# A chunked delta rule on one core: the triangular inverse kept as full 128x128 blocks in place of 64x64 blocks, and a solve as one product in place of three

## The chip, the core and the metric

The kernel runs on one core of one Trainium2 chip. TensorE (PE) multiplies matrices, VectorE (DVE) and ScalarE (ACT) do elementwise work and read its results out of PSUM, GpSimd (POOL) does small elementwise work in SBUF, and SyncE (SP) issues the loads. The metric is the device time of one execution in microseconds; lower is better.

## What is computed

Two layers of a trunk over 256 tokens of width 1024, in float32. Each layer has a SwiGLU block, a mixer and another SwiGLU block, with norms around them. The mixer of layer 0 is a short convolution; that of layer 1 is a gated delta rule with 16 value heads of 128 columns. The part that matters here is the delta rule. The reference works in chunks of 64 tokens:

```
a = where(strict, einsum("bhncd,bhnsd->bhncs", k_beta, k) * decay, 0.0)
t_inv = lax.linalg.triangular_solve(eye + a, broadcast_to(eye, a.shape), left_side=True, lower=True)
u = einsum("bhncs,bhnse->bhnce", t_inv, v_beta)
w = einsum("bhncs,bhnsd->bhncd", t_inv, k_beta * exp(g)[..., None])
...
v_new = u_n - einsum("bhcd,bhde->bhce", w_n, state)
o = einsum("bhcd,bhde->bhce", q_g_n, state) + einsum("bhcs,bhse->bhce", qk_n, v_new)
state = state * exp(gl_n) + einsum("bhcd,bhce->bhde", k_tail_n, v_new)
```

The result doesn't depend on where a chunk ends, so the kernel takes one chunk of 128 tokens: two chunks (t = 0, 1) and 16 heads, in 4 groups (gi) of 4 heads.

## The kernel before

**Products.** The large products are float32, done as two or three products of rounded halves: `unit` loads a 128x1024 piece of a weight (SP), rounds it on ACT (L111, `whi`) and takes the rest on DVE (L113, `wlo`). In the delta mixer `stat_group` (L247 to L249) makes q, k and v, `act_group` (L216, L217, L220) makes the gate z, and `out_proj` (L288 to L290) the last product. The products of the delta rule itself are plain float32 products; in the trace each of them is two passes on PE.

**Order.** Each of these groups calls `tk.tick()` every 6 or 12 matmuls. A ticker then resumes the generators that are due: `kq_chain`, `invert`, `v_pair`, one `scan` for each group gi, and `z_chain`. A generator that yields n is resumed n ticks later, so that its instructions stand between those of the weight products. A scheduler in the compiler then moves a few rows past one that it thinks would wait. An engine runs its list in order.

**The matrix.** `kq_chain` leaves for each gi and t a tile `KQ[gi][t]` of 128x4x2x128 elements: for each of 4 heads the decayed key-key matrix (index 0 of the third axis, upper triangular as stored) and the decayed key-query matrix (index 1). The 32x32 blocks on the diagonal are copied to `Ld`.

**The inverse.** `invert` inverts all 32 x 4 diagonal blocks of 32x32 at once by forward substitution on DVE (L635, L637), which gives them as `Xd` and, transposed, `Yd` (L639, L641). After `INV_WAIT` ticks it goes on in two halves of 16 matrices: 32 products of 32x32 with the block beside the diagonal (L652), a copy (L656, into `T1`), a tick, 32 more products (L663), and then the tiles `Y64[gi]`: the inverses of the 64x64 diagonal blocks, put together from copies of `Yd` and zeros on POOL (L669, L671) and from PSUM on ACT (L673).

**The solve.** `scan(gi)` waits for v and for `Y64[gi]`, and solves twice, for t = 0 and 1, with other products between. `solve` does it by 64x64 blocks: both diagonal blocks (L704, 8 products of 64x64 by 64x128, whose results ACT copies, L706); two ticks; the block beside them (L710, 4 products, ACT copy L713); two ticks; the second diagonal block again (L718, 4 products), subtracted by DVE (L719); two ticks. What follows in `scan` and `intra` (L726, L757, L766) is of 128 rows.

## Time and profile before

| what | value |
|---|---|
| median of three runs | 1145.38 us (1145.0 to 1147.21) |
| the profiled execution, its own time | 1144.5 us |
| span of its profile | 1142.8 us |
| PE busy | 1108.3 us (97%) |
| DVE busy | 759.1 us (66%) |
| ACT busy | 652.4 us (57%) |
| POOL busy | 80.3 us (7%) |
| mean granted TensorE clock | 0.994 of 2.4 GHz |
| mean rate of the loads | 174 GB/s |

The profile is of one execution, and 1.7 us of its time lie outside the span. Matmuls are pipelined: one that is listed with 0.28 us starts 0.12 us after the one before it. What an instruction costs PE is therefore read from the start of one row to the start of the next, in the view in order of time, and not from its length. The inversion and the solves lie between about 815 and 930 us.

### The profile page before, as it was taken

To read this page: it belongs to the slowest core of one execution; us is meant where nothing else is said; L and a number is where in the kernel's file an instruction comes from. 1 tells how busy PE (TensorE), PEld (TensorE's weight loads), DVE (VectorE), ACT (ScalarE), POOL (GpSimd) and SP (SyncE) were. 2 spreads that over 40 slices of the span, in tenths; PEclk is the share of its full clock that TensorE was granted. 3 is DMA by queue.
4 is the path that set the end of the run, shared out by engine and by line. 5 is a ranking of instruction groups with operands and counts; after the bars stand their busy time and mean duration, and the time that the engine had idled before them with its cause. 6 is when DMAs were issued, how large, how long until landed. Compare 5 with 4: busy or idle time off the path is not lost.

```text
span 1142.8 us, 16740 instructions
## 1 busy us (share of the span) xinstructions
PE 1108.3 (97%) x6272; PEld 942.5 (82%) x6272; DVE 759.1 (66%) x1145; ACT 652.4 (57%) x1187; POOL 80.3 (7%) x145
## 2 busy tenths in 40 slices
PE   6999999999999999999999999988999999999997
PEld 5888887788788888788888887867998877888886
DVE  5686735687776764667674479778865567767543
ACT  5766635545565653556563468874676545656432
POOL 1000000000200000010000012210210212000000
PEclk9999999999999999999999999999999999999999
DMA  7765555665566555566655543346434145665552
GB/s 259 232 210 193 195 162 165 225 183 195 176 225 204 174 197 167 175 215 202 200 176 171 183 157 111 95 141 189 146 97 160 43 132 169 221 197 180 189 166 74
DMA packets 55953, 198.64 MB, mean 174 GB/s; under 512 B 6720, under 2 KB 7232, under 8 KB 55872
## 3 DMA queue, kind: packets, MB, share of 16 engines
q1 hardware_dynamic: 55872, 197.58, 53.9%
q8 instruction: 49, 0.80, 0.3%
q14 instruction: 32, 0.26, 0.1%
HBM read 196.51 MB, written 1.05 MB: 173 GB/s over the span
## 4 chain that ended last, share of the span: by engine, by line
PE 81%; DVE 6%; ACT 5%; DMA 3%; issue 2%; POOL 2%; SPq 0%; DVEq 0%; POOLq 0%; ACTq 0%
PE mm L264 27%; PE mm L265 14%; PE acc L288 7%; PE acc L289 7%; PE acc L290 7%; PE mm L216 3%; PE mm L217 3%; PE mm L220 3%; DVE wlo L113 2%; ACT whi L111 1%; DMA raw<-in_gdn_v 1%; ACT blk L611 1%; PE mm L247 1%; DVE kq L545 1%; ACT junk L145 1%
## 5 line engine op out<-in xcount | busy, mean ns | idle before, releaser
L113 DVE TENSOR_TENSOR wlo<-raw,whi 128x1024 fp32r<-128x1024 f32 (+2 forms) x362 | 440.0, 1220 | 234.0 <-ACT whi L111 231.6
L111 ACT ACTIVATE whi<-raw 128x1024 fp32r<-128x1024 f32 (+2 forms) x362 | 379.5, 1053 | 231.4 <-PE acc L290 101.5
L264 PE MATMUL mm<-x,whi 128*128 128x512 f32 x1312 | 462.7, 398 | 0.0
L265 PE MATMUL mm<-x,wlo 128*128 128x256 f32 x1312 | 367.3, 280 | 0.0
L264 PEld LDWEIGHTS mm<-x,whi 128*128 128x128 f32 x1312 | 246.4, 188 | 60.0
L265 PEld LDWEIGHTS mm<-x,wlo 128*128 128x128 f32 x1312 | 247.5, 189 | 0.1
L288 PE MATMUL acc<-whi,hb 128*128 128x512 f32 x352 | 136.9, 389 | 0.0
L289 PE MATMUL acc<-wlo,hb 128*128 128x512 f32 x352 | 135.7, 386 | 0.2 <-DVE wlo L113 0.2
L290 PE MATMUL acc<-whi,hb 128*128 128x512 f32 x352 | 135.6, 385 | 0.0
L273 ACT ACTIVATE corr<-mm 128x256 f32<-128x256 f32 x164 | 62.0, 379 | 85.9 <-PE mm L265 85.9
L217 PE MATMUL mm<-wlo,x 128*128 128x512 f32 (+1 forms) x240 | 94.9, 395 | 1.5 <-DVE wlo L113 1.4
L216 PE MATMUL mm<-whi,x 128*128 128x512 f32 (+1 forms) x240 | 95.3, 398 | 0.7 <-ACT x L173 0.6
L220 PE MATMUL mm<-whi,x 128*128 128x512 f32 (+1 forms) x240 | 88.6, 392 | 0.0
L288 PEld LDWEIGHTS acc<-whi,hb 128*128 128x128 f32 x352 | 66.1, 188 | 14.4 <-issue 1.2
L289 PEld LDWEIGHTS acc<-wlo,hb 128*128 128x128 f32 x352 | 66.1, 188 | 13.5 <-DVE wlo L113 0.5
L290 PEld LDWEIGHTS acc<-whi,hb 128*128 128x128 f32 x352 | 66.1, 188 | 13.4
L151 POOL TENSOR_SCALAR rstd<-ss 128x1 f32<-128x1 f32 x24 | 12.2, 510 | 812.5 <-ACT junk L145 812.5
L247 PE MATMUL mm<-x,whi 128*128 128x256 f32 x200 | 60.0, 300 | 2.0 <-DVE kq L545 2.0
L248 PE MATMUL mm<-x,whi 128*128 128x256 f32 x200 | 58.8, 294 | 0.0
L249 PE MATMUL mm<-x,wlo 128*128 128x256 f32 x200 | 58.5, 292 | 0.0
L217 PEld LDWEIGHTS mm<-wlo,x 128*128 128x128 f32 x240 | 45.7, 190 | 12.2 <-DVE wlo L113 3.8
L216 PEld LDWEIGHTS mm<-whi,x 128*128 128x128 f32 x240 | 45.6, 190 | 11.0 <-ACT x L173 2.3
(209 smaller groups left out, 1237.3 us busy)
## 6 DMA issues: line engine op xcount, KB each, us to landing
raw<-in_w_gu SPq DMA_DIRECT2D x176, 512.0 KB, 4.3
raw<-in_w_dn SPq DMA_DIRECT2D x88, 512.0 KB, 3.6
raw<-in_sc_in SPq DMA_DIRECT2D x24, 512.0 KB, 4.2
raw<-in_gdn_z SPq DMA_DIRECT2D x16, 512.0 KB, 3.7
raw<-in_gdn_v SPq DMA_DIRECT2D x16, 512.0 KB, 4.3
raw<-in_gdn_out SPq DMA_DIRECT2D x16, 512.0 KB, 3.7
gamma<-in_norm_g SPq DMA_DIRECT2D x12, 512.0 KB, 5.9
raw<-in_gdn_a SPq DMA_DIRECT2D x9, 512.0 KB, 4.3
```

Of the source, the lines that this page charges most:

```text
L111: S.activation(hi[:, r], raw[:, r], AF.Copy)
L113: V.tensor_tensor(lo[:, r], raw[:, r], hi[:, r], ALU.subtract)
L216: PE.matmul(pt, lhsT=xh[:, t, k, :], rhs=hi, start=(k == 0), stop=False)
L217: PE.matmul(pt, lhsT=xh[:, t, k, :], rhs=lo, start=False, stop=False)
L220: PE.matmul(pt, lhsT=xl[:, t, j, :], rhs=part(j)[0], start=False, stop=(j == KD - 1))
L247: PE.matmul(ptile, lhsT=hi, rhs=xh[:, :, k, :], start=(k == 0), stop=False)
L264: PE.matmul(pt, lhsT=hi, rhs=xx[:, :, :, k, :], start=(k == 0), stop=False)
L265: PE.matmul(pt[:, 1, :], lhsT=lo, rhs=xx[:, 0, :, k, :], start=False, stop=(k == KD - 1))
L273: S.activation(c, pt[:, 1, :], AF.Copy)
L288: PE.matmul(o, lhsT=yh(c, t), rhs=hi[:, r], start=(c == 0), stop=False)
L289: PE.matmul(o, lhsT=yh(c, t), rhs=lo[:, r], start=False, stop=False)
L290: i = PE.matmul(o, lhsT=yl(c, t), rhs=hi[:, r], start=False, stop=(c == n - 1)).ins
```

## The change

`invert` now also puts together the block of the 128x128 inverse that lies beside its two 64x64 diagonal blocks, and writes the whole inverse over the key-key half of `KQ[gi][t]`. The solve is then one product of 128x128 by 128x128 for each head. In detail:

- Before `INV_WAIT`, POOL copies the 32x32 diagonal blocks from `Yd` into `KQ` (L648 of the changed kernel): 32 copies of 32x4x32.
- For each half POOL builds tiles `E[gi]` (64 columns wide) from `Xd` (L658, 2 copies of 32x8x32 for each gi, and one memset, L659).
- With the second 32x32 products (L677, as L663 before) stand 16 more for each half (L678). ACT copies the results to `E` (L681, one for each gi) and `KQ` (L685, four of 32x4x32 for each gi).
- One tick later: 8 products of 64x64 by 64x64 for each gi (L691), which ACT copies into the upper half of `E` (L693).
- One tick later: 8 more such products for each gi (L698), copied by ACT into `KQ` (L701, two of 64x4x64 for each gi).
- `solve` has 4 products (L730), one ACT copy and one wait of two ticks. Its second and third stage are gone.

```diff
+            for gi in range(NG):
+                for t in range(NT):
+                    for b in range(4):
+                        r = slice(b * B32, (b + 1) * B32)
+                        G.tensor_copy(KQ[gi][t][r, :, 0, r], Yd[r, 8 * gi + t:8 * gi + t + 7:2, :])
             yield INV_WAIT
             for half in range(2):
                 hs = slice(16 * half, 16 * half + 16)
+                gis = (2 * half, 2 * half + 1)
+                E = {}
+                for gi in gis:
+                    E[gi] = slab([P, 8, 64], F32, "E64")
+                    for b in range(2):
+                        r = slice(b * B32, (b + 1) * B32)
+                        G.tensor_copy(E[gi][r, :, r], Xd[r, 8 * gi:8 * gi + 8, :])
+                    G.memset(E[gi][0:B32, :, B32:], 0.0)
...
                         PE.matmul(py[r0, x, :], lhsT=T1[r1, ht, :], rhs=Yd[r1, ht, :], start=True, stop=True)
-                for gi in (2 * half, 2 * half + 1):
-                    y = slab([P, 8, 64], F32, "Y64")
...
-                        G.tensor_copy(y[r, :, (b % 2) * B32:(b % 2 + 1) * B32], Yd[r, g8, :])
-                        if b % 2:
-                            G.memset(y[r, :, 0:B32], 0.0)
-                        else:
-                            S.activation(y[r, :, B32:], py[r, x8, :], AF.Copy, scale=-1.0)
-                    Y64[gi] = y
+                    PE.matmul(py[B32:64, x, :], lhsT=Yd[B32:64, ht, :], rhs=T1[B32:64, ht, :], start=True, stop=True)
+                for gi in gis:
+                    x0 = 8 * (gi % 2)
+                    S.activation(E[gi][B32:64, :, 0:B32], py[B32:64, x0:x0 + 8, :], AF.Copy, scale=-1.0)
+                    for t in range(NT):
+                        for b in (0, 2):
...
+                            S.activation(KQ[gi][t][r0, :, 0, r1], py[r0, x0 + t:x0 + t + 7:2, :], AF.Copy, scale=-1.0)
+                yield 1
+                lo, up = slice(0, 64), slice(64, P)
+                for gi in gis:
...
+                    for x in range(8):
+                        PE.matmul(pz[up, x, :], lhsT=KQ[gi][x % 2][lo, x // 2, 0, up], rhs=E[gi][lo, x, :],
+                                  start=True, stop=True)
+                    S.activation(E[gi][up], pz[up], AF.Copy)
+                yield 1
+                for gi in gis:
...
+                    for x in range(8):
+                        PE.matmul(pw[lo, x, :], lhsT=E[gi][up, x, :], rhs=KQ[gi][x % 2][up, x // 2, 0, up],
+                                  start=True, stop=True)
+                    for t in range(NT):
+                        S.activation(KQ[gi][t][lo, :, 0, up], pw[lo, t:t + 7:2, :], AF.Copy, scale=-1.0)
+                    inv_done[gi] = True
...
         def solve(gi, t, r):
             pu = side_bank()
             for hv in range(4):
-                x = (hv // 2) * 4 + (hv % 2) * 2 + t
-                for rr in (slice(0, 64), slice(64, P)):
-                    PE.matmul(pu[rr, hv, :], lhsT=Y64[gi][rr, x, :], rhs=r[rr, hv, :], start=True, stop=True)
+                PE.matmul(pu[:, hv, :], lhsT=KQ[gi][t][:, hv, 0, :], rhs=r[:, hv, :], start=True, stop=True)
             y = slab([P, 4, P], F32, "ysol")
             S.activation(y, pu, AF.Copy)
-            yield SCAN_WAIT
...
-                PE.matmul(pt[64:, hv, :], lhsT=KQ[gi][t][0:64, hv, 0, 64:], rhs=y[0:64, hv, :],
-                          start=True, stop=True)
...
-            S.activation(tt[64:], pt[64:], AF.Copy)
-            yield SCAN_WAIT
...
-                PE.matmul(px[64:, hv, :], lhsT=Y64[gi][64:, x, :], rhs=tt[64:, hv, :], start=True, stop=True)
-            V.tensor_tensor(y[64:], y[64:], px[64:], ALU.subtract)
             yield SCAN_WAIT
             return y
```

On PE, in the inversion, before (L652 and L663 are the 32x32 products, L247 to L249 those of the weights of v, L688 transposes of v):

```order
L652 MATMUL acc<-blk,KQ 32x32 x32
...
L663 MATMUL acc<-blk 32x32
L652 MATMUL acc<-blk,KQ 32x32 x2
L663 MATMUL acc<-blk 32x32 x31
L652 MATMUL acc<-blk,KQ 32x32 x30
...
L663 MATMUL acc<-blk 32x32
...
L663 MATMUL acc<-blk 32x32 x31
```

And now, from the last of the second 32x32 products of the first half on (L678; the rows left out are weight products: 11, then 3 of which the first is shown, then 9; L716 are the transposes of v):

```order
L678 MATMUL acc<-blk 32x32
...
L691 MATMUL acc<-E_7903,KQ 64x64 x8
L691 MATMUL acc<-E_7907,KQ 64x64 x8
L247 MATMUL mm<-x_5757,whi 128x256
...
L716 MATMUL mm<-ident,yb 128x128 x4
...
L698 MATMUL acc<-KQ,E_7903 64x64 x8
L698 MATMUL acc<-KQ,E_7907 64x64 x8
L666 MATMUL acc<-blk,KQ 32x32 x32
```

Two groups of 16 products of 64x64 each have come in between the halves, each behind a stretch of weight products, and the first products of the second half (L666) have moved from the middle of the second products to behind the new ones. In the other half it is the same.

On PE, the first solves of the groups gi = 0 and 1, before:

```order
L704 MATMUL acc<-nv,Y_7951 64x128 x8
...
L710 MATMUL acc<-ysol,KQ 64x128 x4
L704 MATMUL acc<-nv,Y_7960 64x128 x8
L688 MATMUL mm<-ident,yb 128x128 x4
...
L718 MATMUL acc<-tsol,Y_7951 64x128 x4
L710 MATMUL acc<-ysol,KQ 64x128 x4
...
L726 MATMUL acc<-ysol,KQ 128x128 x4
L718 MATMUL acc<-tsol,Y_7960 64x128 x4
```

And now:

```order
L698 MATMUL acc<-KQ,E_8101 64x64 x8
L698 MATMUL acc<-KQ,E_8105 64x64 x8
L730 MATMUL acc<-nv,KQ 128x128 x8
L716 MATMUL mm<-ident,yb 128x128 x4
...
L739 MATMUL acc<-ysol,KQ 128x128 x8
```

The two solves stand side by side, right behind the end of the inversion, and the next product of the scan (L739, L726 before) follows after 24 weight products in place of 72.

On POOL, in the inversion, before (L669 copies from `Yd`, L671 zeros):

```order
L671 MEMSET Y_7951 32x8x32 x2
L669 COPY Y_7951<-blk 32x8x32 x4
L669 COPY Y_7960<-blk 32x8x32 x2
L671 MEMSET Y_7960 32x8x32
```

And now (L658 copies from `Xd` to `E`, L648 from `Yd` to `KQ`):

```order
L658 COPY E_7903<-blk 32x8x32 x2
L658 COPY E_7907<-blk 32x8x32 x2
L659 MEMSET E_7907 32x8x32
L658 COPY E_8101<-blk 32x8x32
L648 COPY KQ<-blk 32x4x32 x32
L658 COPY E_8101<-blk 32x8x32
L659 MEMSET E_8101 32x8x32
L658 COPY E_8105<-blk 32x8x32 x2
L659 MEMSET E_8105 32x8x32
```

All 32 copies into `KQ` stand ahead of three of the copies that fill the `E` tiles of the second half.

## Rows read from the trace of the kernel before

**Rows 1.** The page: busy time of the engines over the whole span, and the chain of work that ended last, by engine.

```profile
PE 1108.3 (97%) x6272; PEld 942.5 (82%) x6272; DVE 759.1 (66%) x1145; ACT 652.4 (57%) x1187; POOL 80.3 (7%) x145
...
PE 81%; DVE 6%; ACT 5%; DMA 3%; issue 2%; POOL 2%; SPq 0%; DVEq 0%; POOLq 0%; ACTq 0%
```

**Rows 2.** Busy time by stretch, in us: first a stretch of the first layer for comparison, then those from the end of the inversion to the last solve. The columns are PE, weight loads, DVE, ACT, POOL, the granted clock, the share of the DMA engines and GB/s.

```profile
60.00:300.00 240.00, 238.27 (x1222) 201.20 (x1221) 164.71 (x228) 129.42 (x208) 8.02 (x14) 1.00 0.58 189
817.00:830.00 13.00, 12.19 (x313) 10.93 (x311) 9.97 (x15) 10.87 (x22) 9.89 (x21) 1.00 0.49 156
830.00:860.00 30.00, 30.00 (x250) 27.37 (x250) 21.67 (x45) 21.73 (x51) 4.76 (x8) 1.00 0.38 122
860.00:880.00 20.00, 20.00 (x145) 16.49 (x144) 10.75 (x20) 12.79 (x22) 0.00 (x0) 1.00 0.35 108
880.00:900.00 20.00, 20.00 (x132) 15.73 (x130) 8.62 (x22) 8.93 (x34) 4.46 (x9) 1.00 0.24 80
900.00:935.00 35.00, 35.00 (x192) 28.61 (x191) 19.61 (x37) 18.51 (x45) 5.00 (x9) 1.00 0.34 100
```

**Rows 3.** All the waits of PE between 800 and 940 us: us in total, times, longest.

```profile
PE acc L663 <- ACT blk L656: 0.6, 1, 0.6
PE acc L289 <- DVE wlo L113: 0.2, 1, 0.2
PE acc L652 <- DVE blk L639: 0.2, 1, 0.2
```

**Rows 4.** PE in order of time around the first product of a solve (start, length, what).

```profile
829.67 0.28 PE L248 MATMUL mm<-x,whi 128*128 128x256 f32 x1
829.79 0.28 PE L249 MATMUL mm<-x,wlo 128*128 128x256 f32 x1
830.00 1.09 PE L704 MATMUL acc<-nv,Y 64*64 64x128 f32 x16
831.02 0.39 PE L247 MATMUL mm<-x,whi 128*128 128x256 f32 x1
831.24 0.28 PE L248 MATMUL mm<-x,whi 128*128 128x256 f32 x1
```

**Rows 5.** PE in order of time: the third product of one solve beside the second of another, and the last third product, alone.

```profile
839.05 0.76 PE L718 MATMUL acc<-tsol,Y 64*64 64x128 f32 x5
...
840.56 0.39 PE L247 MATMUL mm<-x,whi 128*128 128x256 f32 x1
...
923.47 1.08 PE L718 MATMUL mm<-tsol,Y 64*64 64x128 f32 x8
924.49 0.50 PE L288 MATMUL acc<-whi,hb 128*128 128x512 f32 x1
```

**Rows 6.** PE in order of time: a product of a scan in full 128x128 blocks, of the same shape as the new solve.

```profile
927.36 1.05 PE L726 MATMUL mm<-ysol,KQ 128*128 128x128 f32 x8
928.17 0.48 PE L288 MATMUL acc<-whi,hb 128*128 128x512 f32 x1
928.48 0.40 PE L289 MATMUL acc<-wlo,hb 128*128 128x512 f32 x1
```

**Rows 7.** PE in order of time: the first products of the inversion, of 32x32, and the second ones after their wait.

```profile
817.53 1.20 PE L652 MATMUL acc<-blk,KQ 32*32 32x32 f32 x64 [0.18 <-DVE blk L639]
818.66 0.38 PE L247 MATMUL mm<-x,whi 128*128 128x256 f32 x1
...
821.18 1.10 PE L663 MATMUL acc<-blk 32*32 32x32 f32 x57 [0.63 <-ACT blk L656]
```

**Rows 8.** Single instructions by line: lengths in ns (least, median, most), first and last start, shape. The first two are copies of the inversion, the last two the ACT copy and the DVE subtraction of a solve.

```profile
L656 ACT ACTIVATE blk<-acc x4: 589/590/591, 819.4 to 825.4; 32x512 f32<-32x512 f32 x4
L673 ACT ACTIVATE Y<-acc x8: 356/374/375, 822.6 to 828.4; 32x256 f32<-32x256 f32 x8
...
L713 ACT ACTIVATE tsol<-acc x5: 592/592/594, 835.2 to 875.7; 64x512 f32<-64x512 f32 x5
...
L719 DVE TENSOR_TENSOR ysol<-ysol,acc x4: 691/692/692, 840.2 to 875.2; 64x512 f32<-64x512 f32 x4
```

**Rows 9.** The copies on POOL: all of them (busy us, mean ns, idle before), the first six in order of time, then by stretch one that lay in 820 to 821 us and three in 823 to 824 us (ns: least, median, most); and from DVE's list in order of time the transposition that gives `Xd` and the work beside that one copy.

```profile
L669 POOL COPY Y<-blk 32x256 f32<-32x256 f32 x16 | 9.0, 562 | 62.1 <-DVE blk L641 61.4
...
819.37 4.58 POOL L669 COPY Y<-blk 32x256 f32<-32x256 f32 x6 [61.35 <-DVE blk L641]
...
L669 POOL COPY Y<-blk x1: 1299/1299/1299, 819.8 to 819.8; 32x256 f32<-32x256 f32 x1
...
L669 POOL COPY Y<-blk x3: 391/396/398, 822.7 to 823.6; 32x256 f32<-32x256 f32 x3
...
815.28 2.20 DVE L639 STREAM_TRANSPOSE blk<-blk 128x1024 f32<-128x1024 f32 x1
...
819.50 1.34 DVE L113 TENSOR_TENSOR wlo<-raw,whi 128x1024 fp32r<-128x1024 f32 x1
```

**Rows 10.** A long wait of PE ahead of the inversion (it ended at about 799 us): the wait, and busy time in the 5 us behind it and in 5 us of undisturbed work of the same kind.

```profile
PE mm L688 <- ACT yb L532: 3.8, 1, 3.8
...
800.00:805.00 5.00, 5.00 (x28) 5.00 (x27) 5.00 (x14) 2.64 (x5) 0.00 (x0) 0.56 0.51 134
...
810.00:815.00 5.00, 5.00 (x44) 5.00 (x44) 4.94 (x15) 3.53 (x6) 0.00 (x0) 1.00 0.56 143
```

More of the change, by code (lines that the diff above doesn't have):

```diff
@@ L620, in kq_chain @@
             tk.start(invert())
-        Y64 = [None] * NG
+        inv_done = [False] * NG
         def invert():
@@ L663, in invert @@
                         PE.matmul(py[r0, x, :], lhsT=T1[r1, ht, :], rhs=Yd[r1, ht, :], start=True, stop=True)
[L664 to L674 removed]
+                    PE.matmul(py[B32:64, x, :], lhsT=Yd[B32:64, ht, :], rhs=T1[B32:64, ht, :], start=True, stop=True)
[4 more added lines that the diff above has]
+                        for b in (0, 2):
+                            r0, r1 = slice(b * B32, (b + 1) * B32), slice((b + 1) * B32, (b + 2) * B32)
+                            S.activation(KQ[gi][t][r0, :, 0, r1], py[r0, x0 + t:x0 + t + 7:2, :], AF.Copy, scale=-1.0)
+                yield 1
+                lo, up = slice(0, 64), slice(64, P)
+                for gi in gis:
+                    pz = side_bank().rearrange("p a (b c) -> p (a b) c", c=64)
+                    for x in range(8):
[4 more added lines that the diff above has]
+                for gi in gis:
+                    pw = side_bank().rearrange("p a (b c) -> p (a b) c", c=64)
+                    for x in range(8):
[4 more added lines that the diff above has]
+                    inv_done[gi] = True
         nv = [None] * NG
@@ L701, in solve @@
             for hv in range(4):
-                x = (hv // 2) * 4 + (hv % 2) * 2 + t
-                for rr in (slice(0, 64), slice(64, P)):
-                    PE.matmul(pu[rr, hv, :], lhsT=Y64[gi][rr, x, :], rhs=r[rr, hv, :], start=True, stop=True)
+                PE.matmul(pu[:, hv, :], lhsT=KQ[gi][t][:, hv, 0, :], rhs=r[:, hv, :], start=True, stop=True)
             y = slab([P, 4, P], F32, "ysol")
             S.activation(y, pu, AF.Copy)
-            yield SCAN_WAIT
-            pt = side_bank()
-            for hv in range(4):
-                PE.matmul(pt[64:, hv, :], lhsT=KQ[gi][t][0:64, hv, 0, 64:], rhs=y[0:64, hv, :],
-                          start=True, stop=True)
-            tt = row("tsol")[:, 0:4 * P].rearrange("p (a b) -> p a b", a=4)
-            S.activation(tt[64:], pt[64:], AF.Copy)
-            yield SCAN_WAIT
-            px = side_bank()
-            for hv in range(4):
-                x = (hv // 2) * 4 + (hv % 2) * 2 + t
-                PE.matmul(px[64:, hv, :], lhsT=Y64[gi][64:, x, :], rhs=tt[64:, hv, :], start=True, stop=True)
-            V.tensor_tensor(y[64:], y[64:], px[64:], ALU.subtract)
             yield SCAN_WAIT
```

5 lines of the change are left out of this document (1 added, 4 removed).

## The prediction

> **What bounds the kernel now.** I read the page first. PE is busy for 97% of the span and 81% of the chain that ended last is PE [rows 1], so time is won or lost only where PE's list gets shorter or longer, or waits. The change touches some 115 us of the span. By stretch, PE has work all the time from 830 to 935 us, at the full granted clock, with DVE and ACT 43 to 72% busy and the loads at 80 to 122 GB/s [rows 2]. The list of waits says the same: in 800 to 940 us PE waits 1.0 us in all [rows 3]. So what is taken out of PE's list there is won, until something new makes it wait. The one place with no such room on another engine is 817 to 830, where ACT works 10.87 of 13 us [rows 2]. Prices on PE come from the view in order of time, start to start.
>
> **What the solves give back.** A weight product starts 0.12 us after the one before. The first product of a solve occupies PE from 830.00 to 831.02, and the steps into and out of it are 0.21 and 0.22 us in place of 0.12 [rows 4]: 1.02 us of work and 0.19 for the change of block size. The third product alone takes 1.02 us too (923.47 to 924.49), though it has 8 passes in place of 16: blocks in different places run side by side, and one block's pass costs 0.127 us. Third and second product next to each other take 1.51 us for both [rows 5]. With 8 solves of three products, four such neighbours, and 19 stays in small blocks (counted in the view in order of time): 24 x 1.02 - 4 x 0.5 + 19 x 0.19 = 26.1 us.
>
> The new solve is 8 passes of 128x128 by 128 columns. That is the shape of L726, which takes 0.81 us (927.36 to 928.17) and makes the step behind it about 0.1 longer [rows 6]: 8 x 0.9 = 7.2 us. Ahead of it and behind it stand as many ticks as now; those that go belong to the two stages that go, so no copy gets less cover. **The solves give 18.9 us.** The ACT copies (8 x 0.59) and DVE subtractions (8 x 0.69) that go too [rows 8] lie beside PE and count nothing.
>
> **What the inversion takes.**
> - The 64 products of 64x64 by 64 columns (L691, L698) are 128 passes, one behind the other in the same block. The trace has no such pass. The 32-column pass is one bound: 64 of them, in two places at a time, take 817.53 to 818.66 [rows 7], so 0.035 us each in its place. The 128-column pass, 0.127, is the other. On the line between them 64 columns cost 0.066; I take 0.07, since a pass of a 64-row block loads more than one of 32. That is 9.0 us, between 4.5 and 16.3.
> - The 32 products of L678 are 64 passes of 32 columns. They use the rows of one L677 product and the columns of no other. At the mean step of L652, 1.13 / 64 = 0.018 us, they cost 1.1 us; 0 if they hide beside L677, 2.3 if they queue behind it. The Trainium skill ("TensorE: Matmul & The Clock Gate", back-to-back issue gap) says that starts never come closer than about 25 ns, however few the columns. The rows are closer than that, 0.018 us, and they decide; by the rule L678 would cost 1.6 us as an estimate, and the sum would be half a microsecond less.
> - Stays in small blocks: 4 before, 10 now (two single products stand alone ahead of their groups). 6 x 0.19 = 1.1 us.
>
> **That is 11.2 us, and 7.7 us less on PE in all.**
>
> **Waits that may come.** The wait for `T1` in the first half, 0.63 us [rows 7], stays: the rows that stood beside it before didn't shorten it. The new stages wait on ACT and POOL. On ACT the inversion's copies grow from 8 x 0.37 to 12 x 0.37 (L681, and L701, which has the same 256 elements), 16 smaller ones of at most 0.37 (I take 0.28) and 4 x 0.59: from 3.0 to about 11.3 us [rows 8]. The stretch grows from 13 to about 28 us on PE. With the copies into `T1` (2.4) and the other work, which was 10.87 - 5.4 = 5.5 us in 13 and so some 12 in 28, ACT has about 26 of 28 us to do. It fits, barely, and ACT runs its list in order. In front of each new group, though, PE has 10 to 15 weight rows, 1.3 to 2 us, and the first group of products needs only the first copies; I follow the lists to margins of 0.2 to 1 us at the second `T1`, L691 and L698. I count **1.5 us of waits**, between 0 and 5: twice the wait that stands there now, and a little for POOL (below). The scans start two ticks later and each needs eight fewer, so the last gate is ready earlier than now, and nobody waits for that.
>
> The sum is 7.7 - 1.5 = 6.2 us less. Against the profiled execution's own 1144.5 us that is 1138.3; the median of the runs is 0.9 higher, so I forecast **1139.2 us**. Its own range, from the ends of these terms, is 1132 to 1143.
>
> **Rivals.**
> - *POOL holds the inversion.* The matrix isn't ready before POOL has written the diagonal blocks into `KQ`, and the `E` tiles of the second half come behind them. POOL can start when `Xd` is there, at 817.5 us. By the prices above PE comes to the second half of L698 at about 830, which needs 21 copies, and to the second L691 at about 837, which needs 38. So the copies must take under 0.6 and 0.51 us on average. Undisturbed copies of twice the size take 0.39; one that lay beside DVE's L113 took 1.30, and the first six took 4.58, 0.76 each [rows 9]. I expect smaller copies at no more than 0.39 and three or four of them held for 0.9 us: 38 x 0.39 + 3.6 = 18.4 us, in time by a microsecond; at the mean of 0.56 now, 1.9 us of wait, inside the term above. At 0.76 throughout, POOL would be done at 846.4 and PE would have waited 9.4 us. After a wait of 3.8 us the granted clock was 0.56 for 5 us, and PE did 28 rows in place of 44 [rows 10], so 1.9 us more: 7.7 less and 11.3 more, **1149.0 us**, slower than before. It decides from about 0.67 us a copy. The Trainium skill ("SBUF — State Buffer", SBUF: two separate sides) has a rule for it: VectorE with two SBUF inputs and GpSimd share a pair of ports, and whichever starts first holds it for its whole instruction. The pairing of the 1.30 us copy with L113 agrees. That only L113 is such work, and that it ran three times in 13 us, speaks against it.
> - *A 64-column pass costs as much as a 128-column one*, because the load of a block's weights or the way through it sets the step. Then L691 and L698 cost 16.3 in place of 9.0: 6.2 - 7.3, or 1.1 us more, **1146.5 us**. For it: the 128-column pass in a 64x64 block (0.127) is slower than in a full one (0.81 / 8 = 0.101), so something beside the columns counts. Against it: the 32-column pass at 0.035 shows that columns count most.
> - *The freed time is lost to weights.* The weights of the gate and of the last product must come in up to 19 us less. L289 waits 0.2 us for its rounding once already [rows 3]. If each of its 16 pieces waited so, 3.5 us would go: **1142.7 us**. Against it: in 60 to 300 us the same path brings 189 GB/s with PE 99% busy, against 80 to 122 here [rows 2].
>
> That the change doesn't do what it says is excluded: the order shows four products for each solve.
>
> **How the numbers follow.** Forecast 0.73, weights 0.08, equal passes 0.10, POOL 0.09. A measurement of this kernel can tell 0.2%, 2.3 us, from no change, so 1143.1 and 1147.7 are the borders. Faster: 0.70 of the forecast and 0.05 of the weights, 0.75. Slower: POOL and a little of the equal passes, 0.10. The same: 0.15. The range takes in the upper end of the forecast and the equal passes, and leaves out POOL and the lowest microsecond: 1133 to 1146.5.
>
> **What would show it.** In the profile after: L730 about 0.8 to 0.9 us for each solve, and no other product of 64-row blocks behind the inversion; L691 and L698 1.1 us for 8 products; L678's groups with L677 at about 1.7 us; PE's waits between 817 and 845 under 3 us, on ACT; POOL's 32 copies done before 837. PE busy should fall by about 8 us. It is wrong if the passes of L691 take over 0.11 us, if a wait of PE names POOL with over 2 us, or if a new wait on L113 stands in the last product.

## The result and the profile after

| | before | after |
|---|---|---|
| device time, median (lowest to highest) | 1146.3 us (1145.0 to 1147.3) | 1135.04 us (1132.7 to 1137.4) |
| ratio to before, 95% interval | | 0.9904 (0.9887 to 0.9921) |
| span of the profiled execution | 1142.8 us | 1130.9 us |
| first 32x32 product to last transposition at L171 | 817.5 to 961.5: 144.0 us | 815.1 to 949.5: 134.4 us |
| from there to the end | 181.3 us | 181.4 us |

The kernel is faster by 11.3 us; 6.2 were forecast. In the table's fourth line, called the stretch from here on, is all the work that the change touches. It is 9.6 us shorter, and what lies behind it is as long as before. The remaining 2.4 us of the two profiled executions lie ahead of the stretch, in code that is the same. They are no part of the change: the changed kernel's second profiled execution, below, started its stretch at 818.3, and the other kernels below start theirs between 814.8 and 823.2.

The page, by the rows that answer to [rows 1]:

```profile
PE 1097.5 (97%) x6272; PEld 937.8 (83%) x6272; DVE 753.2 (67%) x1137; ACT 654.7 (58%) x1203; POOL 87.6 (8%) x165
...
PE 81%; DVE 6%; ACT 5%; DMA 3%; issue 2%; POOL 2%; SPq 0%; DVEq 0%; POOLq 0%; ACTq 0%
```

PE is busy 10.8 us less, so the gain is work that is no longer on PE's list. Busy time by stretch, with the columns of [rows 2]:

```profile
817.00:830.00 13.00, 12.64 (x271) 11.79 (x271) 7.48 (x13) 11.41 (x28) 11.60 (x31) 1.00 0.39 124
830.00:845.00 15.00, 14.89 (x234) 13.88 (x233) 9.11 (x18) 12.81 (x28) 4.46 (x8) 1.00 0.48 142
...
860.00:880.00 20.00, 20.00 (x123) 17.70 (x122) 13.38 (x27) 15.91 (x47) 4.29 (x7) 1.00 0.38 127
...
900.00:935.00 35.00, 34.01 (x165) 27.80 (x162) 19.70 (x24) 18.40 (x32) 3.99 (x7) 1.00 0.48 150
```

Through the inversion (the first two rows) ACT works 24.2 of 28 us, and PE hardly waits for it. The list of PE's waits between 800 and 940 us, as [rows 3]:

```profile
PE mm L171 <- DVE xs L164: 0.7, 1, 0.7
PE acc L677 <- ACT blk L670: 0.4, 1, 0.4
PE acc L289 <- DVE wlo L113: 0.3, 1, 0.3
PE acc L666 <- DVE blk L640: 0.2, 1, 0.2
```

The L171 row is the norm at the end of the stretch, which has moved into this window. The other three are the waits of before. The list of the waits of the weight loads, from 830 to 840 us, has a new one:

```profile
PEld acc L691 <- POOL E L659: 0.3, 1, 0.3
```

PE in order of time at the new products, first a group of L691 between weight products, then the end of L698 and the first L730, which here stands for two solves:

```profile
821.20 0.28 PE L249 MATMUL mm<-x,wlo 128*128 128x256 f32 x1
821.41 2.08 PE L691 MATMUL acc<-E,KQ 64*64 64x64 f32 x32
823.41 0.39 PE L247 MATMUL mm<-x,whi 128*128 128x256 f32 x1
...
834.43 0.38 PE L247 MATMUL mm<-x,whi 128*128 128x256 f32 x1
834.92 1.14 PE L691 MATMUL acc<-E,KQ 64*64 64x64 f32 x16
...
838.70 0.86 PE L698 MATMUL acc<-KQ,E 64*64 64x64 f32 x12
839.49 2.05 PE L730 MATMUL acc<-nv,KQ 128*128 128x128 f32 x16
841.37 0.49 PE L716 MATMUL mm<-ident,yb 128*128 128x128 f32 x3
```

Start to start, 32 passes of L691 take 2.00 us, 0.0625 each, and 16 passes of L730 take 1.88, 0.94 a solve. Pass by pass, L691 starts every 0.058 us; the rest of its 2.00 lies at the two ends of the group. POOL in order of time, and then the 32 copies from the view of one line (ns: least, median, most):

```profile
817.25 1.29 POOL L658 COPY E<-blk 32x256 f32<-32x256 f32 x1
818.49 12.53 POOL L648 COPY KQ<-blk 32x128 f32<-32x128 f32 x32
...
831.87 2.63 POOL L658 COPY E<-blk 32x256 f32<-32x256 f32 x2
834.56 0.30 POOL L659 MEMSET E<- 32x256 f32 x1
```

```profile
L648 POOL COPY KQ<-blk x32: 284/288/1192, 818.5 to 830.7; 32x128 f32<-32x128 f32 x32
```

The last block of the second half's `E` is finished at 834.86, and the load of L691's weights, which waited for it, starts 0.05 us later. So PE already stands for POOL here. Its weight product of 834.43 is followed after 0.49 us, where steps out of one small block and into another come to 0.22 + 0.09 = 0.31 [rows 4]: it lost about 0.2 us.

**Where the 9.5 us are.** All of PE's products in the stretch, each counted from its start to the next one's start, summed by line (so a product carries the wait or step behind it; "solves" are the kernel before's three products and the changed kernel's one):

| products | before | after | difference |
|---|---|---|---|
| solves (L704, L710, L718; L730) | 22.2 | 7.1 | -15.1 |
| 32x32 products of the inversion | 5.3 | 4.9 | -0.4 |
| L691, L698 | | 8.2 | +8.2 |
| weight products beside the inversion (L247 to L249) | 20.1 | 21.5 | +1.4 |
| the scans' other products and transpositions | 23.8 | 21.5 | -2.3 |
| last product (L288 to L290) | 47.5 | 46.3 | -1.3 |
| the gate's products (L216, L217, L220), L171 and L341 | 25.0 | 25.1 | 0.0 |
| sum | 143.9 | 134.4 | -9.5 |

### The profile page after: what moved, and what is told of

Read it like the earlier page. It is cut to its first block, busy times and chain, and to the rows that moved or that the text cites. A ratio compares the mean times of both kernels' runs of the same rounds, so it can differ in the third digit from the quotient of the medians.

```text
span 1130.9 us, 16772 instructions
## 1 busy us (share of the span) xinstructions
PE 1097.5 (97%) x6272; PEld 937.8 (83%) x6272; DVE 753.2 (67%) x1137; ACT 654.7 (58%) x1203; POOL 87.6 (8%) x165
## 4 chain that ended last, share of the span: by engine, by line
PE 81%; DVE 6%; ACT 5%; DMA 3%; issue 2%; POOL 2%; SPq 0%; DVEq 0%; POOLq 0%; ACTq 0%
PE mm L264 27%; PE mm L265 14%; PE acc L289 8%; PE acc L290 8%; PE acc L288 8%; PE mm L216 3%; PE mm L217 3%; PE mm L220 3%; DVE wlo L113 2%; ACT whi L111 1%; ACT blk L611 1%; DVE kq L545 1%; PE mm L171 1%; ACT junk L145 1%; DMA raw<-in_gdn_v 1%
## 5 line engine op out<-in xcount | busy, mean ns | idle before, releaser
L113 DVE TENSOR_TENSOR wlo<-raw,whi 128x1024 fp32r<-128x1024 f32 (+2 forms) x362 | 441.0, 1222 | 229.8 <-ACT whi L111 227.8
L288 PE MATMUL acc<-whi,hb 128*128 128x512 f32 x352 | 136.5, 388 | 0.0
L289 PE MATMUL acc<-wlo,hb 128*128 128x512 f32 x352 | 135.6, 385 | 0.3 <-DVE wlo L113 0.3
L290 PE MATMUL acc<-whi,hb 128*128 128x512 f32 x352 | 135.4, 385 | 0.0
L216 PE MATMUL mm<-whi,x 128*128 128x512 f32 (+1 forms) x240 | 95.6, 399 | 0.4 <-ACT x L173 0.3
L217 PE MATMUL mm<-wlo,x 128*128 128x512 f32 (+1 forms) x240 | 95.0, 396 | 0.7 <-DVE wlo L113 0.5
L220 PE MATMUL mm<-whi,x 128*128 128x512 f32 (+1 forms) x240 | 89.0, 393 | 0.0
L289 PEld LDWEIGHTS acc<-wlo,hb 128*128 128x128 f32 x352 | 66.1, 188 | 13.7 <-DVE wlo L113 0.8
L288 PEld LDWEIGHTS acc<-whi,hb 128*128 128x128 f32 x352 | 66.1, 188 | 13.4
L290 PEld LDWEIGHTS acc<-whi,hb 128*128 128x128 f32 x352 | 66.1, 188 | 13.3
L247 PE MATMUL mm<-x,whi 128*128 128x256 f32 x200 | 59.3, 297 | 2.0 <-DVE kq L545 2.0
L249 PE MATMUL mm<-x,wlo 128*128 128x256 f32 x200 | 57.6, 288 | 0.0
L217 PEld LDWEIGHTS mm<-wlo,x 128*128 128x128 f32 x240 | 45.8, 191 | 11.1 <-DVE wlo L113 2.4
L216 PEld LDWEIGHTS mm<-whi,x 128*128 128x128 f32 x240 | 45.7, 191 | 10.8 <-ACT x L173 2.0
```

The costliest lines, as they stand in the source:

```text
L113: V.tensor_tensor(lo[:, r], raw[:, r], hi[:, r], ALU.subtract)
L216: PE.matmul(pt, lhsT=xh[:, t, k, :], rhs=hi, start=(k == 0), stop=False)
L217: PE.matmul(pt, lhsT=xh[:, t, k, :], rhs=lo, start=False, stop=False)
L220: PE.matmul(pt, lhsT=xl[:, t, j, :], rhs=part(j)[0], start=False, stop=(j == KD - 1))
L247: PE.matmul(ptile, lhsT=hi, rhs=xh[:, :, k, :], start=(k == 0), stop=False)
L288: PE.matmul(o, lhsT=yh(c, t), rhs=hi[:, r], start=(c == 0), stop=False)
```

## Experiments

Each kernel is compared with the kernel before on the same chip. The stretch is the one of the table above, read from the profiled execution: 144.0 before, 134.4 after. Two kernels were traced twice, and their stretches agree within 0.1 us (134.4 and 134.5, and 130.8 twice).

**The new solve alone.** The inversion of the kernel before, and a solve of one product, which multiplies by the key-key block as it stands (what would turn it into an inverse is left out):

```diff
-                x = (hv // 2) * 4 + (hv % 2) * 2 + t
-                for rr in (slice(0, 64), slice(64, P)):
-                    PE.matmul(pu[rr, hv, :], lhsT=Y64[gi][rr, x, :], rhs=r[rr, hv, :], start=True, stop=True)
+                PE.matmul(pu[:, hv, :], lhsT=KQ[gi][t][:, hv, 0, :], rhs=r[:, hv, :], start=True, stop=True)
...
-                PE.matmul(pt[64:, hv, :], lhsT=KQ[gi][t][0:64, hv, 0, 64:], rhs=y[0:64, hv, :],
...
-                PE.matmul(px[64:, hv, :], lhsT=Y64[gi][64:, x, :], rhs=tt[64:, hv, :], start=True, stop=True)
```

> The inversion as before, with its 64x64 tiles, and only the solve as one product with the key-key half of KQ as it stands, so that the inverse it multiplies by is not one: the copies and products that would make it are left out. I compare the stretch from the first 32x32 product of the inversion to the last transposition behind the mixer's output product: 144.0 us before, 134.4 in the changed kernel. Theory (a solve costs what its products occupy on PE): the 18.9 us of the prediction, so 125.1 us, and a time of about 1127 us. Rival (freed time is lost to weights): waits of PE on the rounding of weights (L113) of 3 us or more, and 128.6 us.

Measured: 1131.17 us, ratio 0.9874 (0.9846 to 0.9902), stretch 127.3, which is 16.7 less. The mechanism is there, with a size 2.2 under the theory's. By the count start to start the solves' own products give 14.5 (22.2 to 7.7). One solve waits for DVE, and the gate's products take 0.8 longer than before (22.6 to 23.4), two of them held near the end of the stretch:

```profile
PE mm L702 <- DVE rsol L757: 0.4, 1, 0.4
```

The rival's 3 us of waits on L113 aren't there; the longest is 0.3.

**The new inversion alone.** The changed inversion, with `Y64` and the three-product solve of before beside it:

```diff
+                for gi in gis:
+                    y = slab([P, 8, 64], F32, "Y64")
+                    g8, x8 = slice(8 * gi, 8 * gi + 8), slice(8 * (gi % 2), 8 * (gi % 2) + 8)
+                    for b in range(4):
+                        r = slice(b * B32, (b + 1) * B32)
+                        G.tensor_copy(y[r, :, (b % 2) * B32:(b % 2 + 1) * B32], Yd[r, g8, :])
...
+                    Y64[gi] = y
```

> The full inversion of the changed kernel, the 64x64 tiles beside it, and the solve in three products as before (its second product reads a block that is overwritten, so its values are not the reference's). The same stretch, 144.0 us before. Theory from the rows of the changed kernel (8.1 us of 64x64 products, 1.1 for six more stays in small blocks, the third 32x32 products free, no new wait): 153.2 us, about 1155 us. Rival, the sum on record (11.2 us and 1.5 of waits): 156.7 us. If ACT or POOL hold the inversion, with the copies of both, it is more and PE's waits name them.

Measured: 1165.45 us, ratio 1.0167 (1.0134 to 1.0201), stretch 164.2, which is 20.2 more. Both numbers missed. A wait shows why: PE's list of waits, POOL in order of time, and busy time in and behind the wait, with the columns of [rows 2].

```profile
PE acc L703 <- POOL E L660: 4.1, 1, 4.1
```

```profile
836.08 0.83 POOL L692 COPY Y<-blk 32x256 f32<-32x256 f32 x2
...
838.42 0.82 POOL L659 COPY E<-blk 32x256 f32<-32x256 f32 x2
839.30 0.30 POOL L660 MEMSET E<- 32x256 f32 x1
```

```profile
835.00:845.00 10.00, 6.58 (x44) 6.02 (x45) 0.97 (x3) 4.88 (x15) 8.34 (x24) 0.62 0.31 99
845.00:855.00 10.00, 10.00 (x107) 9.30 (x107) 2.52 (x4) 5.74 (x12) 0.00 (x0) 0.87 0.17 52
```

Here POOL makes the blocks of `Y64` ahead of the second half's `E`, and PE stands still for them. In the 10 us that hold the wait the granted clock is 0.62 on average, and 0.87 in the next 10. That is the rival of the prediction in which POOL holds the inversion, so this kernel didn't tell the inversion's own price. The run with three products (below) does.

**Without the third 32x32 products.** L678 goes, and its block of `E` stays zero; ACT copies a piece of L677's result, of the same size, to another block in its place:

```diff
-                    PE.matmul(py[B32:64, x, :], lhsT=Yd[B32:64, ht, :], rhs=T1[B32:64, ht, :], start=True, stop=True)
...
-                    S.activation(E[gi][B32:64, :, 0:B32], py[B32:64, x0:x0 + 8, :], AF.Copy, scale=-1.0)
+                    S.activation(E[gi][0:B32, :, B32:], py[0:B32, x0:x0 + 8, :], AF.Copy, scale=-1.0)
```

> The changed kernel without the third 32x32 products (L678): the block that they make is left at zero, and ACT copies another one of the same size in their place. Theory (they hide beside the others): the stretch stays at 134.4 us, within 0.2. Rival on record (they cost 0.018 us a pass): 133.3 us.

Measured: 1136.13 us, stretch 134.8, which is 0.4 over the changed kernel's where the theory allowed 0.2. The 0.4 isn't in the inversion: its 32x32 products take 4.85 us by the count, and 4.87 with L678. It lies in the gate's products near the end of the stretch (23.1 in place of 22.5), where one waits 0.2 us for DVE's L113. So the 64 passes of L678 cost nothing. PE in order of time:

```profile
821.88 1.19 PE L677 MATMUL acc<-blk 32*32 32x32 f32 x62 [0.36 <-ACT blk L670]
823.00 0.39 PE L248 MATMUL mm<-x,whi 128*128 128x256 f32 x1
```

62 passes take 1.12 us. In the changed kernel 94 passes, with L678's among them, take 1.13 (818.78 to 819.91).

**Products of half the columns.** Each 64x64 product of L691 and L698 is made as two of 32 columns, 256 passes in place of 128:

```diff
-                        PE.matmul(pz[up, x, :], lhsT=KQ[gi][x % 2][lo, x // 2, 0, up], rhs=E[gi][lo, x, :],
-                                  start=True, stop=True)
+                        for c in (slice(0, B32), slice(B32, 64)):
+                            PE.matmul(pz[up, x, c], lhsT=KQ[gi][x % 2][lo, x // 2, 0, up], rhs=E[gi][lo, x, c],
+                                      start=True, stop=True)
```

> The changed kernel with each of the 64x64 products as two of 32 columns: 256 passes in place of 128. Theory (columns set the step; 0.035 us for 32 columns): 9.0 us in place of 8.1, the stretch 135.3 us. Rival on record (a pass costs the same whatever its columns): 16 us in place of 8.1, the stretch 142.4 us.

Measured: 1153.2 us, ratio 1.0058 (1.0039 to 1.0077), stretch 151.6. PE in order of time, and busy time in the first group, behind it and in the second:

```profile
829.21 3.92 PE L692 MATMUL acc<-E,KQ 64*64 64x32 f32 x64
833.05 0.79 PE L719 MATMUL mm<-ident,yb 128*128 128x128 f32 x4
```

```profile
829.30:833.00 3.70, 3.70 (x64) 3.70 (x64) 1.67 (x3) 2.89 (x9) 3.30 (x9) 1.00 0.71 196
833.50:836.30 2.80, 2.80 (x14) 2.61 (x12) 1.11 (x3) 1.46 (x4) 2.45 (x9) 0.50 0.13 45
836.50:840.30 3.80, 3.80 (x64) 3.80 (x64) 0.14 (x1) 0.65 (x2) 3.24 (x11) 0.95 0.00 0
```

At full clock a pass of 32 columns takes 3.84 / 64 = 0.060 us, and one of 64 columns took 0.0625; inside the groups both start every 0.058. In a block of 64 rows, then, half the columns save nothing, and the 256 passes took 16.3 us by the count start to start where the 128 took 8.2. The theory had them at 9.0; the rival's price is the measured one. It accounts for 8.1 of the 17.2 us. The rest is the clock: it was 0.50, the lower of its two levels (1.2 of 2.4 GHz), between the groups of short products though PE had no idle time. By the count the weight products beside the inversion take 5.3 us more there, the solves 1.7 and the 32x32 products 1.5, and PE has no new wait. That effect neither side had named.

**POOL's copies twice.**

```diff
-                        G.tensor_copy(KQ[gi][t][r, :, 0, r], Yd[r, 8 * gi + t:8 * gi + t + 7:2, :])
+                        for _ in range(2):
+                            G.tensor_copy(KQ[gi][t][r, :, 0, r], Yd[r, 8 * gi + t:8 * gi + t + 7:2, :])
```

> The changed kernel with each of the 32 GpSimd copies of a diagonal block made twice (the same values again). Theory (the rival that GpSimd holds the inversion is real, the changed kernel only stands just short of it): the copies took 12.53 us for 32, and the second half's two other blocks were done 0.1 to 0.4 us before L691 asked for them, so with 12.5 us more the second half waits: TensorE shows a wait of 10 to 12.5 us on a GpSimd block ahead of the second L691 or the second L698, the clock falls behind it (2 to 4 us more), the stretch from the first 32x32 product to the last transposition is 146 to 151 us where the changed kernel has 134.4, and the time is 1147 to 1152. Rival (TensorE has other work to go on with, and GpSimd's time is free up to twice its load): 134.4, 1135, and no wait on GpSimd.

Measured: 1153.77 us, ratio 1.0063 (1.005 to 1.0076), stretch 152.5. PE's waits and busy time:

```profile
PE acc L699 <- POOL KQ L649: 4.1, 2, 2.4
PE acc L692 <- POOL E L660: 1.8, 1, 1.8
```

```profile
825.00:835.00 10.00, 5.90 (x64) 5.36 (x63) 2.23 (x5) 4.37 (x12) 8.48 (x29) 0.86 0.30 95
835.00:845.00 10.00, 10.00 (x189) 9.24 (x188) 2.45 (x2) 6.28 (x13) 8.68 (x25) 0.50 0.23 64
```

PE waits for POOL, as the theory had it, but for 5.9 us and not for 10 to 12.5. The granted clock is 0.50 for 10 us behind the first wait, so that PE comes to the second half late itself. The stretch grew by 18.1, which leaves some 12 us to the clock, not 2 to 4: twice what the waits cost. (This 12 is what is left of the sum; it wasn't measured by itself.)

**Both halves in one round.** The first 32x32 products of both halves stand together, then the second and third, then L691, then L698; POOL makes `E` first and the lower diagonal blocks of `KQ` before the upper. `pzmm` and `pwmm` are the products of L691 and L698, `pwev` the copies of L701:

```diff
+            for bb in ((2, 3), (0, 1)):
+                for gi in range(NG):
+                    for t in range(NT):
+                        for b in bb:
+                            r = slice(b * B32, (b + 1) * B32)
+                            G.tensor_copy(KQ[gi][t][r, :, 0, r], Yd[r, 8 * gi + t:8 * gi + t + 7:2, :])
...
+            for gi in range(NG):
+                pz = bank64()
+                for x in range(8):
+                    pzmm(pz, gi, x)
+                S.activation(E[gi][up], pz[up], AF.Copy)
+            yield 1
+            for gi in range(NG):
+                pw = bank64()
+                for x in range(8):
+                    pwmm(pw, gi, x)
+                pwev(pw, gi)
```

> The changed kernel with both halves of the inversion taken through each step together: four steps (128 first 32x32 passes, 192 of the second and third, 64 of L691, 64 of L698) in place of eight, with the GpSimd copies in the order in which they are asked for (the blocks beside, then the lower diagonal blocks, then the upper). Same passes, half as many stays. Theory (each stay costs TensorE 0.1 to 0.4 us of its neighbours: the 12 weight products behind a block took 1.49 to 1.62 us beside 1.44 elsewhere, and the wait on the T1 copy with its broken block 0.5 us): 1 to 2 us less, stretch 132.4 to 133.4. Rival (long rows of short products lower the clock, as they did with products of half the columns): the granted clock falls below 0.9 behind the 64 passes and the stretch is 138 us or more.

Measured: 1134.18 us, ratio 0.9897 (0.9881 to 0.9912), stretch 133.1, 1.3 less than the changed kernel's and as the theory had it. The clock stayed at 1.00 through 64 passes of L698 in a row (3.87 us) and behind them. So this long row of short products didn't lower it; the one with half the columns did.

**L691 and L698 side by side.** As before, and with the second half's L691 put between the first half's L698, product by product:

```diff
+                for x in range(8):
+                    pzmm(pz, gi + 2, x)
+                    pwmm(pw, gi, x)
```

> As the kernel with one round, but the second half's L691 products stand between the first half's L698 products, one by one: they use opposite quarters of the array. Five steps. Theory (a pass of 64 rows by 64 columns took 0.0625 us at 64 columns and 0.060 at 32, so what it pays is a price of its own quarter that is not its columns; two in opposite quarters run beside each other, as L704's did at 0.0605 each where L718's alone took 0.115): the 64 mixed passes take 2.0 to 2.2 us in place of 4.0, so 2 us less than without, and with the stays 2.5 to 3.5 us less than the changed kernel: stretch 131 to 132. Rival (the price is of the pass in the instruction queue or the load, one at a time for the whole array): the mixed passes stay at 0.0625 us each and the stretch is 133 to 133.9.

Measured: 1132.92 us, ratio 0.9881 (0.9868 to 0.9893), stretch 130.8. PE in order of time, at both ends of the mixed group:

```profile
831.93 0.28 PE L249 MATMUL mm<-x,wlo 128*128 128x256 f32 x1
832.14 0.33 PE L696 MATMUL acc<-E,KQ 64*64 64x64 f32 x2
...
834.34 0.28 PE L700 MATMUL acc<-KQ,E 64*64 64x64 f32 x2
834.54 0.39 PE L247 MATMUL mm<-x,whi 128*128 128x256 f32 x1
```

The 64 mixed passes take 2.40 us, 0.0375 each. One behind the other they took 4.0. The group is 0.2 over the theory's 2.2, and the stretch 0.2 under its 131 to 132. In the group one step is 0.3 us long, where a weight load waits for a copy of POOL; in the repeat of this kernel (the last run below), which has no such wait, the same 64 passes take 2.01 us:

```profile
830.20 0.27 PE L696 MATMUL acc<-E,KQ 64*64 64x64 f32 x1
...
832.21 0.38 PE L247 MATMUL mm<-x,whi 128*128 128x256 f32 x1
```

Inside it a pass of L696 and one of L700 start in every 0.058 us, where one of them alone started before. So the price of a short pass is paid in its own quarter of the array, and another quarter can work meanwhile.

**V_WAIT 7 and INV_WAIT 40.**

```diff
-INV_WAIT = 37
-V_WAIT = 4
+INV_WAIT = 40
+V_WAIT = 7
```

> The changed kernel with V_WAIT 7 in place of 4 and INV_WAIT 40 in place of 37: the transpositions of a pair come three groups of weight products later, and the inversion keeps its distance. Ahead of the change's stretch TensorE waits 4.2 us for the ACT result of L532 at L716, and its clock is 0.91 behind it. Theory (that wait is one of order alone): it goes, and the program is 3 to 5.5 us shorter, 1130 to 1132. Rival (VectorE is the bound there, 18.96 of 20 us busy from 780 to 800 and 19.07 from 800 to 820): the time goes into waits on the weights' lower parts (L113) or on the transposed blocks (L640) ahead of the first 32x32 product, and the time stays within 1 us of the changed kernel's.

Measured: 1150.14 us, ratio 1.0031 (1.0018 to 1.0045), stretch 149.8. Neither side foresaw it. The wait at L716 is gone, but the scheduler now puts the 32 copies into `KQ` ahead of all `E` blocks on POOL. PE's waits, and POOL in order of time:

```profile
PE acc L691 <- POOL E L659: 9.6, 1, 9.6
...
PE mm L716 <- ACT yb L532: 0.3, 1, 0.3
```

```profile
819.25 14.65 POOL L648 COPY KQ<-blk 32x128 f32<-32x128 f32 x32 [61.73 <-DVE blk L642]
833.97 0.83 POOL L658 COPY E<-blk 32x256 f32<-32x256 f32 x2
```

Of what POOL makes, L691 needs only `E`, and copies that it doesn't need stand in front of it. This is the POOL rival again, brought about by two numbers elsewhere.

**The same two numbers with products side by side,** where the code sets POOL's order.

> The kernel with L691 and L698 side by side (1132.9), with V_WAIT 7 and INV_WAIT 40 as well. Theory (in the run with V_WAIT 7 alone the wait at L716 fell from 4.2 to 0.3 us and TensorE was busy for all of 780 to 800; the time was lost only because GpSimd made the blocks beside behind the 32 copies, which this kernel's order in the code rules out): no wait on GpSimd, no wait at L716 over 1 us, the first 32x32 product no later than at 818, the stretch 130 to 132, and 1127 to 1131. Rival (VectorE sets the start of the stretch): the stretch starts at 820 or later, and 1132 to 1134.

Measured: 1133.41 us, ratio 0.989 (0.9869 to 0.9912), stretch 132.2, begun at 819.7. There is no wait on POOL and none at L716, and the time is within 0.5 us of the kernel without the two numbers, inside the rival's 1132 to 1134 and outside the theory's 1127 to 1131. So what is saved at L716 isn't kept. Part of it goes into the stretch, which is 1.4 longer than without the two numbers, with waits that weren't there:

```profile
PE acc L696 <- ACT E L685: 1.3, 1, 1.3
PE acc L679 <- ACT blk L670: 1.2, 2, 0.9
```

The rest would be a start that comes no sooner. One trace doesn't show that, since the start differs by several microseconds from kernel to kernel. That DVE sets it was argued from its busy time and not tried by itself.

**The changed inversion with three products for a solve,** which take their blocks from `KQ`:

```diff
-                PE.matmul(pu[:, hv, :], lhsT=KQ[gi][t][:, hv, 0, :], rhs=r[:, hv, :], start=True, stop=True)
+                for rr in (slice(0, 64), slice(64, P)):
+                    PE.matmul(pu[rr, hv, :], lhsT=KQ[gi][t][rr, hv, 0, rr], rhs=r[rr, hv, :], start=True, stop=True)
...
+                PE.matmul(px[64:, hv, :], lhsT=KQ[gi][t][64:, hv, 0, 64:], rhs=tt[64:, hv, :], start=True, stop=True)
```

> The changed kernel's inversion as it is, and the solve of the kernel before with its three products, which take their 64x64 blocks from KQ, so that GpSimd has no more to do than in the changed kernel. Its middle product reads the block that the inversion has written over, so the output is not the reference's. Theory (the parts add: the new solve saves 16.7 us as measured by itself, and the inversion costs what is left of the changed kernel's 9.6, which is 7.1): stretch 144.0 + 7.1 = 151.1, between 150 and 152, and 1151 to 1154. By the prediction's terms (inversion 11.2 and waits 1.5): stretch 156.7. Rival (the inversion costs more beside the old solve than beside the new, as the first run of it by itself said with 20.2): 158 or more with no wait on GpSimd.

Measured: 1158.22 us, ratio 1.0109 (1.0091 to 1.0128), stretch 156.1, 12.1 over the kernel before. The theory that the parts add fell; the sum by the prediction's terms, 156.7, came nearest. PE's waits, and a second and a third product in order of time:

```profile
PE acc L289 <- DVE wlo L113: 1.3, 2, 1.1
PE acc L737 <- DVE rsol L798: 1.3, 1, 1.3
```

```profile
846.07 1.96 PE L737 MATMUL acc<-ysol,KQ 64*64 64x128 f32 x16
...
851.02 1.96 PE L744 MATMUL acc<-tsol,KQ 64*64 64x128 f32 x16
```

Two solves now run in step, so that two second products, in the same place of the array, stand next to each other (16 passes, 1.89 us from 846.07 to the next weight product), where a third and a second product had stood side by side [rows 5]. Start to start, second and third products cost 15.6 in place of 14.4 us. Two waits add 2.4 (L289's was 0.2 before), weight products beside the inversion 1.5, and the inversion's own products 7.6.

**The changed kernel, and the one with products side by side, once more,** beside each other.

> The changed kernel once more, on the same chip and in the same rounds as the one with side by side products. Theory (the gain is the stretch's 9.6 us; what its profiled run had beyond that, an earlier start of the stretch by 2.4 us, changes from run to run and is not the change's): stretch 134.0 to 134.8 again wherever it starts, ratio to the kernel before 0.990 to 0.992. Rival (the change also moves the start): start at 814 to 816 again, ratio below 0.989.

> The kernel with L691 and L698 side by side once more, beside the changed kernel. Theory: its stretch is again 130.5 to 131.2, and its median 2.5 to 4.5 us under the changed kernel's of the same rounds. Rival (the start of the stretch moves by more than that from run to run): the stretch is shorter, and the medians lie within 1.5 us of each other.

Measured: 1136.85 us for the changed kernel, ratio 0.9919 (0.9897 to 0.9941), stretch 134.5, begun at 818.3; 1132.05 us with side by side products, ratio 0.9873 (0.9851 to 0.9895), stretch 130.8. The first theory held. The second held for the stretch, and its medians lie 4.8 us apart where it had 2.5 to 4.5. The version with the products side by side beats both kernels: by 15.1 us the one before, by 4.8 the changed one.

## Why the prediction came out as it did

The sign and the mechanism were right: PE is the bound, its list got shorter, and next to nothing new makes it wait. The size was off by 3.3 us in the stretch (6.2 forecast, 9.5 by the count), and it was off in the terms of what the change adds.

- **The solves, 18.9.** Measured in this kernel: 15.1 from the solves' products, for which the terms are 24 x 1.02 - 4 x 0.5 - 8 x 0.9 = 15.3; and 3.5 from the products around them, which have fewer steps into small blocks beside them (-2.3 in the scans and -1.3 in the last product), for which the term is 19 x 0.19 = 3.6. At the edges themselves the trace says the same: 34 products there that stood next to a small block took 3.8 us over their usual step, and one product stands so now, with 0.1. A solve costs 7.1 / 8 = 0.89, forecast 0.9. This part held in each term.
- **L691 and L698, 9.0.** Measured 8.2. The pass is 0.0625 us, forecast 0.07 between 0.035 and 0.127. That the number was near is luck, since its reason doesn't hold: the line between the 32- and the 128-column pass takes it that columns count all the way. In a 64-row block, 32 columns cost 0.060 and 64 cost 0.0625. The 0.035 belonged to a block of 32 rows. The Trainium skill ("TensorEngine Tiling (Array Packing)", Instruction Overhead) states that a matmul of one column has the same latency as one of 60, and the prediction left it out. The half-column run agrees with it in kind, between 32 and 64 columns, and not in size: the page speaks of about 60 cycles, and a step of 0.058 us at 2.4 GHz is some 140. What sets the 0.058 stays open. Each pass loads its own weights, and PEld was as busy as PE there (3.70 of 3.70 us), so the load may set it; no run took the load away.
- **L678, 1.1.** Measured nothing, by the run without it: the lower bound of the three was the right one. The starts of L677 and L678 come 0.012 us apart (1.13 / 94). The Trainium skill's rule ("TensorE: Matmul & The Clock Gate", back-to-back issue gap) was weighed against 0.018 in the prediction and turned down; the trace of the changed kernel is further from it still.
- **Six more stays, 1.1.** The weight products beside the inversion cost 1.4 more, of which 0.2 is the wait for POOL. The size held.
- **Waits, 1.5.** There are 0.2 us, for POOL at the second half's L691. The wait for `T1` is 0.4 where it was 0.6, and the margins that the prediction followed on ACT all held. It put ACT at 26 of 28 us; it was 24.2.

So 1.5 for waits (the 0.2 is counted with the stays), 1.5 for the 32x32 products (1.1 that weren't due, 0.4 that the `T1` wait and the rest gave) and 0.8 for the passes were counted too much. That is 3.8, less 0.3 each by which solves and stays were short: 3.2, the miss to within a rounding. The medians' difference of 11.3 has 1.7 more than the stretch. In the run once more it was 10.3 with the same stretch, so that part of it at least is scatter of the runs.

**The rivals.**
- *POOL holds the inversion* did happen, for about 0.2 us at the second half's L691; the forecast had POOL in time by a microsecond. The price of the copies was right: half of those into `KQ` took 0.288 or less, a few were held, and the 38 copies of the forecast were done 16.4 us after the first (at 831.47), where it had 18.4. But the second half's L691 stands in two groups, and the second group needs two more copies and a memset, which the forecast left out. Both copies were held (2.63 us from 831.87, beside two L113). The Trainium skill ("SBUF — State Buffer", SBUF: two separate sides) was named for this; the trace agrees, since the `E` copy that took 1.29 us from 817.25 lies beside an L113 that ran from 817.08 for 1.20. Three runs show the rival's mechanism at work (the new inversion alone, POOL's copies twice, V_WAIT 7). They also show that its price was set too low: the prediction put the clock behind a wait at 1.9 us (28 rows in place of 44 in 5 us give 1.8), and with 5.9 us of waits in two places it was about 12.
- *Equal passes* is refuted for 64 against 128 columns. For 32 against 64 it is true. Where between 64 and 128 the columns begin to count stays open. Its argument, that a 128-column pass costs 0.127 in a 64x64 block and 0.101 in a full one, was a misreading: inside the groups they start every 0.109 and 0.111 us, and the difference lies at the groups' ends.
- *Freed time lost to weights*: L289 waits 0.3 us once, as before.

**What the prediction didn't have** is that the two parts depend on each other. The new solve gives 16.7 us with the old inversion and 156.1 - 134.4 = 21.7 with the new one; the new inversion costs 12.1 with the old solve and 134.4 - 127.3 = 7.1 with the new. The traces account for these 5 us. The one with three products shows 2.4 us of waits on DVE that the shorter solve doesn't have, and second and third products that no longer stand beside each other, 1.2. The other 1.5 lie in the run of the new solve alone: there the solves take 7.7 us by the count and the gate's products 23.4, with the held products named above, and in the changed kernel 7.1 and 22.5. The forecast's 12.7 for the inversion with its waits is close to what it costs beside the old solve, and the changed kernel never pays that.

## What to carry to other kernels

Price a small product by its block before its columns: in a 64x64 block a pass of 32 columns cost here what one of 64 cost, and what it costs is paid in its own part of the array. Two such groups that use opposite parts belong next to each other, product by product (here 4.0 us became 2.4, and 2.0 in the repeat).

Where a side engine fills blocks that TensorE will read, put in the code which blocks come first. Here the order was left to a scheduler, TensorE already waited 0.2 us for it, and a change of two numbers elsewhere turned a gain of 11 us into a loss of 4. Look for such a wait in the list of the weight loads too: PE's own list didn't have it.

Parts of a change that were measured each by itself needn't add, even with the same engine as the bound: take what a part is worth from a pair of kernels that differ in it alone and have the rest as it will be.

## What the runs showed of the hardware

- A pass of a 64x64 block took 0.060 us with 32 columns and 0.0625 with 64 at full clock, and 0.127 with 128 (alone, before). Without the groups' ends the steps are 0.058, 0.058 and 0.109. Passes in opposite quarters, taken in turn, took 0.0375 each, and 0.031 in the repeat.
- Passes of 32x32 blocks in three places started 0.012 us apart on average.
- The granted clock fell to 0.50 while PE had no idle time at all, behind 64 passes of 32 columns in a 64-row block. Behind 64 passes of 64 columns it stayed at 1.00.
- Waits of 5.9 us in two places left the granted clock at 0.50 for long enough to cost about 12 us; the wait of 3.8 us in the kernel before had cost 1.8 by [rows 10].
- A weight load that waited for POOL started 0.05 us after POOL's last write had ended, in the changed kernel (a wait of 0.3 us) and with V_WAIT 7 (9.8 us).
- A copy of 32x128 elements on POOL took 0.288 us at the median, one of 32x256 took 0.394, and either took 1.2 to 1.3 where it lay beside DVE's L113.
